# Seven quarter products for eight in the layer-0 gate and up projections of a two-layer diffusion backbone

## The chip, the core and the metric

The kernel runs on one core of one Trainium2 chip. The metric is the time of one execution on the device in microseconds (us). The time before is 2477.42 us, the median of three runs (2466.64 to 2477.6).

The core's engines are called by their short names in the profile: PE is TensorE (matmuls; PEld are its weight loads), DVE is VectorE, ACT is ScalarE, POOL is GpSimd, SP is the engine that issues most transfers here. All of them read and write the on-chip memory SBUF; matmuls write to PSUM.

## The reference, cut to what matters

Two layers work on a residual of 1024 features for 512 main tokens and, in layer 0, 256 context tokens. Each layer norms the residual with a modulation that depends on the conditioning, mixes tokens in three branches, merges them, and ends with a SwiGLU feed-forward network (FFN) of 2816 hidden features:

```python
sh1, sc1, g1, sh2, sc2, g2 = jnp.split(sc @ w_ada[l] + b_ada[l], 6, axis=-1)
h = rmsnorm(x, norm1_g[l]) * (1.0 + sc1) + sh1
y, yc = hybrid_mixer(h, hc, w_in[l], ..., w_branch[l], w_out[l], need_ctx)
x = x + g1 * y
h = rmsnorm(x, norm2_g[l]) * (1.0 + sc2) + sh2
x = x + g2 * ((jax.nn.silu(h @ w_gate) * (h @ w_up)) @ w_down)
```

In layer 0 the same is done for the context tokens, with the same weights; in layer 1 only the main tokens go on. Everything is float32.

## The kernel before

**Matmuls.** Features lie on the 128 partitions and tokens along the columns: 768 columns in layer 0 (512 main, 256 context), 512 in layer 1. To keep float32 accuracy, each operand is split in a high and a low part of a narrower type, and a product is three matmuls: high by high, high by low, low by high. `dense` (L290) makes one output tile of 128 features: it loops over the input tiles `k` (eight for 1024 features) and the three part products, and each of these is one matmul of 512 columns and, in layer 0, a second one of 256 columns, because a PSUM bank holds 512. A gate tile in layer 0 is thus 8 x 3 x 2 = 48 matmuls.

**Weights.** `load_raw` (L275) has SP load a weight tile of up to 128 x 1024 numbers into one of three raw buffers (`wr`, L110). `load_w` (L280) splits it: ScalarE copies the high part (L286, into one of two `wh` buffers), VectorE subtracts (L287, into one of two `wl` buffers). A raw buffer is free again when both have read it, a `wh` or `wl` buffer when the last matmul with it is done. The split of the next tile therefore runs beside the matmuls of this one.

**Order of work.** The order on each engine is made ahead by a scheduler from the program order, with dependences and buffers; it may move an instruction ahead of another on the same engine that is not ready in its estimate. On the chip each engine then works through its list in order. SBUF space for activations comes from 27 pages, each for two row blocks of 768 columns (`Pages`, L61; `pair` takes a whole page, `single` a half), handed out in program order by an estimate of TensorE's clock that `spent` (L316) advances.

**FFN.** `layer` (L1071) runs the FFN in four pieces of 5, 5, 6 and 6 hidden tiles (`FF_PIECES`, L30). For each hidden tile of a piece it makes the gate tile, takes its silu on ScalarE (L1176), makes the up tile, multiplies on VectorE (L1178) and splits the result in high and low parts (`gu`, L576 and L577). The piece ends with eight down products, each over the tiles of the piece, whose result is added to the residual X on VectorE (`add_res`, L624), main and context tokens apart. In the last piece the two token blocks are done one after the other. When the first block is done, `settle` (L500) norms it for what follows while the second block's down products run: squares (ScalarE) and their sums (GpSimd and VectorE, L496), a matmul with ones (L458), a power on GpSimd (L468), spreading over the partitions (L482), and then for each feature tile a scaled copy and its high and low parts (L537 to L547).

**Modulation.** `ada_units` (L371) makes four feature tiles of the modulation vectors in four steps. A step loads 512 KB of `w_ada` through the same three raw buffers and accumulates on VectorE (L368; the first product of a unit on ScalarE, L366); the fourth step folds the result (L343, L344). A double unit serves main and context conditioning, a single one the main one alone. The steps wait in a queue; `fill(n)` (L445) puts n of them at a place in the program, `drain` all that are left. Layer 0's own units 4 to 11 are made during its mixer. At the end of layer 0's merge (L1145) the queue gets layer 1's four double units 0 to 3 (16 steps) and its eight single units 4 to 11 (32 steps). One step follows each hidden tile (L1185) and each down product (L1196) of layer 0's FFN.

**Merge.** Before the FFN, each of 3 x 8 merge steps makes a sigmoid gate tile (`w_in`, 1024 features in) and a branch tile (`w_branch`, 512 features in), and adds their product to `macc` (VectorE for the first branch, then also GpSimd, L1138). `fill(1)` follows each; in layer 1 the queue is empty by then.

## Time and profile before

| what | value |
|---|---|
| median of the runs | 2477.42 us |
| profiled execution, from its first to its last instruction | 2460.2 us |
| PE busy | 2410.8 us (98%) |
| VectorE busy | 1426.7 us (58%) |
| ScalarE busy | 837.1 us (34%) |
| GpSimd busy | 202.6 us (8%) |
| granted TensorE clock, mean | 0.998 |

The profile is of one execution. It has no time of its own beside the span of its instructions; the median of the runs lies 17.2 us above it. Times in the trace are counted from the span's start. A stage row gives a stretch, its length, and then for each engine the busy time with the number of instructions in brackets, followed by the granted clock, the share in which the transfer engines were busy, and GB/s. A group row gives line, engine and operation, output and inputs by the program's names, the shape, the count, busy time and mean duration in ns, and then the engine's idle time before them with what ended it. A row of the order in time gives start, duration, engine and line. Matmul durations overlap their neighbours, so the distance of two starts is what one costs.

### The profile page before, as it was taken

What the parts mean: (1) busy time and instruction counts of PE and PEld (TensorE: products, weight loads), DVE (VectorE), ACT (ScalarE), POOL (GpSimd) and SP (SyncE); (2) the same over time, 40 slices, a digit from 0 to 9 for tenths busy, and PEclk for the clock granted to TensorE, in tenths of its full rate; (3) what the DMA queues carried; (4) which work ended last, traced back from release to release, by engine and by line L of the source; (5) the groups of instructions that cost most, each with busy time, mean ns of one, the idle gap of its engine ahead of it and who ended that gap; (6) DMA issues with size and microseconds to landing.
All of it is one profiled execution on the core that took longest, in us unless ns stands there. A gap on an engine that the chain in (4) does not pass through costs nothing. (4 is left out here: it accounts for less than half of the span.)

```text
span 2460.2 us, 34161 instructions
## 1 busy us (share of the span) xinstructions
PE 2410.8 (98%) x13814; PEld 2074.5 (84%) x13814; DVE 1426.7 (58%) x2452; ACT 837.1 (34%) x1372; POOL 202.6 (8%) x143
## 2 busy tenths in 40 slices
PE   8999999999999999999999999999999999999998
PEld 3888888888888888888888888888888889888888
DVE  4688777875454374745353376668884337434335
ACT  3333344442222342221222253324453335322224
POOL 0000100000111210000000040101000122000001
PEclk9999999999999999999999999999999999999999
DMA  8222111123433243434344351112113335233334
GB/s 293 71 78 78 52 42 37 31 60 108 146 112 90 82 127 97 136 98 144 94 122 118 90 150 58 39 42 60 50 51 107 107 102 160 80 102 101 94 101 131
DMA packets 361869, 236.33 MB, mean 96 GB/s; under 512 B 8112, under 2 KB 333168, under 8 KB 361712
## 3 DMA queue, kind: packets, MB, share of 16 engines
q1 hardware_dynamic: 357776, 221.57, 30.5%
q0 software_dynamic: 2304, 10.49, 1.3%
q8 instruction: 109, 1.79, 0.3%
q10 hardware_dynamic: 1632, 2.10, 0.3%
q14 instruction: 48, 0.39, 0.0%
HBM read 226.78 MB, written 7.34 MB: 95 GB/s over the span
## 5 line engine op out<-in xcount | busy, mean ns | idle before, releaser
L286 ACT ACTIVATE wh<-wr 128x1024 fp32r<-128x1024 f32 (+2 forms) x364 | 344.7, 947 | 1042.7 <-PE pd L304 962.1
L287 DVE TENSOR_TENSOR wl<-wr,wh 128x1024 fp32r<-128x1024 f32 (+2 forms) x364 | 396.3, 1089 | 255.4 <-ACT wh L286 251.8
L304 PE MATMUL pd<-hh,wh 128*128 128x512 f32 (+1 forms) x1504 | 456.6, 359 | 1.0 <-DVE X L624 0.8
L304 PE MATMUL pd<-hh,wl 128*128 128x512 f32 (+1 forms) x1504 | 446.5, 353 | 0.3 <-DVE wl L287 0.3
L304 PE MATMUL pd<-hl,wh 128*128 128x512 f32 (+1 forms) x1504 | 443.9, 351 | 0.0
L304 PE MATMUL pd<-fl,wh 128*128 128x512 f32 (+1 forms) x1072 | 322.3, 352 | 0.0
L304 PE MATMUL pd<-fh,wl 128*128 128x512 f32 (+1 forms) x1072 | 321.8, 351 | 0.3 <-DVE wl L287 0.3
L304 PE MATMUL pd<-fh,wh 128*128 128x512 f32 (+1 forms) x1072 | 321.1, 351 | 0.6 <-ACT silu L1176 0.6
L304 PEld LDWEIGHTS pd<-hh,wl 128*128 128x128 f32 x1504 | 246.7, 188 | 37.6 <-DVE wl L287 0.8
L304 PEld LDWEIGHTS pd<-hl,wh 128*128 128x128 f32 x1504 | 246.5, 189 | 34.0
L304 PEld LDWEIGHTS pd<-hh,wh 128*128 128x128 f32 x1504 | 247.4, 189 | 31.3 <-ACT wh L286 1.2
L368 DVE SCALAR_TENSOR_TENSOR acc<-wra,sc,acc 128x512 f32<-128x512 f32 x224 | 162.1, 755 | 190.5 <-DMA wra<-in_w_ada 140.8
L304 PEld LDWEIGHTS pd<-fh,wl 128*128 128x128 f32 x1072 | 177.6, 188 | 30.0 <-DVE wl L287 1.2
L304 PEld LDWEIGHTS pd<-fh,wh 128*128 128x128 f32 x1072 | 176.9, 188 | 29.3 <-ACT silu L1176 0.8
L304 PEld LDWEIGHTS pd<-fl,wh 128*128 128x128 f32 x1072 | 177.4, 188 | 28.0
L304 PE MATMUL pd<-guh,wl 128*128 128x512 f32 (+1 forms) x576 | 174.8, 340 | 1.1 <-DVE wl L287 1.1
L304 PE MATMUL pd<-guh,wh 128*128 128x512 f32 (+1 forms) x576 | 175.0, 340 | 0.0
L304 PE MATMUL pd<-gul,wh 128*128 128x512 f32 (+1 forms) x576 | 174.5, 339 | 0.0
L1178 DVE TENSOR_TENSOR silu<-pd,silu 128x768 f32<-128x768 f32 (+1 forms) x44 | 36.2, 824 | 164.8 <-PE pd L304 164.8
L624 DVE SCALAR_TENSOR_TENSOR X<-pd,mod,X 128x256 f32<-128x256 f32 (+1 forms) x128 | 65.9, 546 | 94.7 <-PE pd L304 94.6
L304 PEld LDWEIGHTS pd<-guh,wl 128*128 128x128 f32 x576 | 99.5, 189 | 14.2 <-DVE wl L287 1.8
L304 PEld LDWEIGHTS pd<-gul,wh 128*128 128x128 f32 x576 | 99.5, 189 | 12.5
(224 smaller groups left out, 3362.0 us busy)
## 6 DMA issues: line engine op xcount, KB each, us to landing
wr<-in_w_in SPq DMA_DIRECT2D x116, 512.0 KB, 3.8
wra<-in_w_ada SPq DMA_DIRECT2D x80, 512.0 KB, 3.7
wr<-in_w_ffn_gate SPq DMA_DIRECT2D x44, 512.0 KB, 3.8
wr<-in_w_ffn_up SPq DMA_DIRECT2D x44, 512.0 KB, 3.9
wr<-in_w_ffn_down SPq DMA_DIRECT2D x48, 384.0 KB, 3.4
wr<-in_w_out SPq DMA_DIRECT2D x32, 512.0 KB, 4.1
wr<-in_w_branch SPq DMA_DIRECT2D x48, 256.0 KB, 2.8
wr<-in_w_ffn_down SPq DMA_DIRECT2D x32, 320.0 KB, 3.1
```

Source lines behind the costliest of these rows:

```text
L286: nc.scalar.activation(out=h, in_=r, func=AF.Copy)
L287: nc.vector.tensor_tensor(out=o, in0=r, in1=h.bitcast(F32), op=ALU.subtract)
L304: nc.tensor.matmul(ps[:, b0:b1], lhsT=w[:, k, :], rhs=x[:, b0:b1], start=b not in first, stop=(k == kt - 1 and i == 2), skip_group_check=True)
L368: nc.vector.scalar_tensor_tensor(out=acc[:, 0:512], in0=w, scalar=sc, in1=acc[:, 0:512], op0=ALU.mult, op1=ALU.add)
L624: self.nc.vector.scalar_tensor_tensor(out=self.X[m][:, c0:c1], in0=ps[:, c0:c1], scalar=gcol(b, m), in1=self.X[m][:, c0:c1], op0=ALU.mult, ...
L1178: nc.vector.tensor_tensor(out=s[:, 0:tt], in0=pu[:, 0:tt], in1=s[:, 0:tt], op=ALU.mult)
```

## The change

For 20 of the 22 hidden tiles of layer 0's FFN, two neighbouring output tiles are made together, with the input features split in two halves of 512 and the tokens in two halves of 384 (`H`). A 2 x 2 by 2 x 2 block product needs eight quarter products; the change uses the scheme with seven, which needs sums of weight quarters and of activation quarters. A quarter product is 4 x 3 = 12 matmuls of 384 columns.

```diff
-FF_PIECES = (5, 5, 6, 6)
+FF_PIECES = ((4, 4, 4, 4, 4, 2), (5, 5, 6, 6))
+FF_PLAIN = 2
+H = T // 2
...
+    def high_low(self, parts):
+        hi = self.wh.tile([P, KD, P], F32R, tag="wh", name=self.nm("wh"))
+        lo = self.wl.tile([P, KD, P], F32R, tag="wl", name=self.nm("wl"))
...
+            self.nc.scalar.activation(out=h, in_=src, func=AF.Copy)
+            self.nc.vector.tensor_tensor(out=l, in0=src, in1=h.bitcast(F32), op=ALU.subtract)
...
+    def seven_acts(self, act):
...
+        for k in range(KD // 2):
...
+            r1, r2 = self.single("b1"), self.single("b2")
+            for r, h, l in ((r1, h1, l1), (r2, h2, l2)):
+                nc.gpsimd.tensor_tensor(out=r[:, 0:T], in0=h[:, 0:T].bitcast(F32), in1=l[:, 0:T].bitcast(F32),
+                                        op=ALU.add)
...
+            nc.vector.tensor_tensor(out=n1, in0=r1[:, 0:H], in1=r1[:, H:T], op=ALU.subtract)
+            nc.vector.scalar_tensor_tensor(out=n2, in0=r2[:, H:T], scalar=-1.0, in1=n1, op0=ALU.mult,
+                                           op1=ALU.subtract)
+            nc.vector.tensor_tensor(out=t3, in0=r2[:, H:T], in1=r1[:, H:T], op=ALU.subtract)
+            nc.vector.scalar_tensor_tensor(out=t4, in0=n2, scalar=-1.0, in1=r2[:, 0:H], op0=ALU.mult,
+                                           op1=ALU.subtract)
...
+            self.split(n[:, 0:T], nh[:, 0:T], nl[:, 0:T])
+            self.split(t3, t3p[:, 0:H], t3p[:, H:T])
...
+        yield None
+        for k, (t, t4) in enumerate(last):
+            h1, l1 = act[k]
+            self.split(t4, h1[:, H:T], l1[:, H:T])
...
+    def product(self, out, w, k0, xs, start):
...
+        for k in range(KD // 2):
+            xh, xl = xs[k]
+            for i, (a, x) in enumerate(((wh, xh), (wh, xl), (wl, xh))):
+                nc.tensor.matmul(out, lhsT=a[:, k0 + k, :], rhs=x, start=first, stop=(k == KD // 2 - 1 and i == 2),
+                                 skip_group_check=True)
...
+    def seven(self, w1, w2, q, take):
...
+        r1, r2 = (self.load_raw(w, KD).rearrange("p k c -> p (k c)") for w in (w1, w2))
...
+        for o, x, y in ((s1, r2[:, 0:n], r2[:, n:2 * n]), (s2, s1, r1[:, 0:n]), (s3, r1[:, 0:n], r2[:, 0:n]),
+                        (s4, s2, r1[:, n:2 * n])):
+            nc.gpsimd.tensor_tensor(out=o, in0=x, in1=y, op=ALU.add)
...
+        g1 = self.high_low([r1])
+        self.product(al, g1, 0, q["B11"], True)
+        nc.scalar.copy(out=u1, in_=al)
+        self.product(be, g1, KD // 2, q["B21"], True)
+        take(0, 0, be, u1)
+        g2 = self.high_low([s21])
+        self.free(sa)
+        self.product(al, g2, 0, q["N2"], False)
+        nc.scalar.copy(out=u2, in_=al)
+        self.product(ga, g2, KD // 2, q["N1"], True)
+        nc.scalar.copy(out=u5, in_=ga)
+        g3 = self.high_low([s34])
+        self.free(sb)
+        self.product(al, g3, 0, q["T3"], False)
+        take(1, 1, al, u5)
+        self.product(ga, g3, KD // 2, q["B22"], False)
+        take(0, 1, ga, u2)
+        g4 = self.high_low([r2[:, n:2 * n]])
+        self.product(al, g4, 0, q["T4"], False)
+        take(1, 0, al, None)
...
+        if l == 1:
+            self.ada_queue += self.ada_units(1, (4, 5, 6, 7), 1) + self.ada_units(1, (8, 9, 10, 11), 1)
...
-                self.fill(1)
+                self.fill(1 + l)
             self.free(*brheld)
         self.free(*hheld)
+        self.drain()
         if l == 0:
-            self.drain()
-            self.ada_queue += self.ada_units(1, (0, 1, 2, 3), 2) + self.ada_units(1, range(4, 12), 1)
+            self.ada_queue += self.ada_units(1, (0, 1, 2, 3), 2)
...
+                if l == 0 and i == 0:
+                    making = self.seven_acts(act2)
+                    next(making)
+                self.fill(0 if l == 0 else 1)
+            if l == 0:
+                if quarters is None:
+                    quarters, qheld = next(making)
+                self.seven_gate_up(l, range(max(f0, plain), f0 + n, 2), quarters, gu, guheld)
```

In words: the first two hidden tiles are made as before (`FF_PLAIN`). After the first, `seven_acts` forms the activation quarters: for each of four pairs of input tiles two GpSimd sums of 768 columns, four VectorE operations of 384, and splits in high and low parts. The quarter T4 is written over the second token half of the first four input tiles once the plain tiles are done.

`seven` (one call for the gate, one for the up of each pair of tiles) loads both raw weight tiles, has GpSimd make four sums of 512 columns, splits four sets of weights (three of 1024 columns and one of 512) and issues the seven products, sets 1 to 3 for two products each and the fourth for the last. Partial results that are used twice are copied from PSUM by ScalarE (`u1`, `u2`, `u5`). `take` is `gate` or `up` inside the new `seven_gate_up`: for the gate, three VectorE additions of 384 columns and four silus; for the up, three additions and four multiplications on VectorE. The split of the pair's results into `gu` stays as it was.

Layer 0's FFN now has six pieces of 4, 4, 4, 4, 4 and 2 tiles, so 48 down products instead of 32, each over fewer tiles. No modulation step follows a hidden tile there any more; the 16 double steps of layer 1 follow the down products. The 32 single steps of layer 1 move to its own merge, two after each merge step.

More of the change, by code (lines that the diff above doesn't have):

```diff
@@ L336, in finish_chains @@
             self.step_chain()
+    def high_low(self, parts):
+        hi = self.wh.tile([P, KD, P], F32R, tag="wh", name=self.nm("wh"))
+        lo = self.wl.tile([P, KD, P], F32R, tag="wl", name=self.nm("wl"))
+        o = 0
+        for src in parts:
+            n = src.shape[1]
+            h, l = (t.rearrange("p k c -> p (k c)")[:, o:o + n] for t in (hi, lo))
+            self.nc.scalar.activation(out=h, in_=src, func=AF.Copy)
+            self.nc.vector.tensor_tensor(out=l, in0=src, in1=h.bitcast(F32), op=ALU.subtract)
+            o += n
+        return hi, lo
@@ new lines, in product @@
+    def product(self, out, w, k0, xs, start):
+        nc = self.nc
+        wh, wl = w
+        first = start
+        for k in range(KD // 2):
[3 more added lines that the diff above has]
+                                 skip_group_check=True)
+                first = False
+            self.spent(3 * (H / 2400 + 0.0133))
@@ new lines, in seven_gate_up, with combine, gate, up @@
+    def seven_gate_up(self, l, tiles, q, gu, guheld):
+        nc, a = self.nc, self.a
+        col = lambda name, i: a[name][l][:, i * P:(i + 1) * P]
+        for i in tiles:
+            s = self.pair("silu")
+            def combine(out, t, h, x, y):
+                if (t, h) == (1, 1):
+                    nc.vector.scalar_tensor_tensor(out=out, in0=x, scalar=-1.0, in1=y, op0=ALU.mult, op1=ALU.subtract)
+                else:
+                    nc.vector.tensor_tensor(out=out, in0=x, in1=y, op=ALU.add)
+            def gate(t, h, x, y):
+                o = s[:, t, h * H:(h + 1) * H]
+                if y is None:
+                    nc.scalar.activation(out=o, in_=x, func=AF.Silu, scale=-1.0)
+                    return
+                combine(o, t, h, x, y)
+                nc.scalar.activation(out=o, in_=o, func=AF.Silu)
+            def up(t, h, x, y):
+                o = s[:, t, h * H:(h + 1) * H]
+                if y is None:
+                    nc.vector.scalar_tensor_tensor(out=o, in0=x, scalar=-1.0, in1=o, op0=ALU.mult, op1=ALU.mult)
+                    return
+                combine(y, t, h, x, y)
+                nc.vector.tensor_tensor(out=o, in0=y, in1=o, op=ALU.mult)
+            for name, take in (("w_ffn_gate", gate), ("w_ffn_up", up)):
+                self.seven(col(name, i), col(name, i + 1), q, take)
+            hp, lp = self.pair("guh", F32R), self.pair("gul", F32R)
+            guheld.extend([hp, lp])
+            for t in (0, 1):
+                self.split(s[:, t, 0:T], hp[:, t, 0:T], lp[:, t, 0:T])
+                gu.append((hp[:, t, :], lp[:, t, :]))
+            self.free(s)
@@ L1166, in layer @@
         f0 = 0
-        for pi, n in enumerate(FF_PIECES):
-            last = pi == len(FF_PIECES) - 1
+        pieces = FF_PIECES[l]
+        plain = FF_PLAIN if l == 0 else 2 * D_FF
+        quarters = qheld = None
+        for pi, n in enumerate(pieces):
+            last = pi == len(pieces) - 1
             gu, guheld = [], []
-            for i in range(n):
+            for i in range(min(n, max(0, plain - f0))):
                 c0 = (f0 + i) * P
@@ L1184, in layer @@
                 gu.append((hp[:, i % 2, :], lp[:, i % 2, :]))
-                self.fill(1)
+                if l == 0 and i == 0:
[6 more added lines that the diff above has]
+                self.seven_gate_up(l, range(max(f0, plain), f0 + n, 2), quarters, gu, guheld)
             if last:
                 self.free(*hheld)
+                if l == 0:
+                    self.free(*qheld)
             if last and l == 0:
```

31 lines of the change are left out of this document (added).

## The prediction

> **What bounds the kernel now.** I read the page first, then the busy time by stage, the order in time inside a stage, and the groups by shape. The first page lines say who is always busy.
>
> ```profile
> span 2460.2 us, 34161 instructions
> PE 2410.8 (98%) x13814; PEld 2074.5 (84%) x13814; DVE 1426.7 (58%) x2452; ACT 837.1 (34%) x1372; POOL 202.6 (8%) x143
> ```
>
> TensorE (PE) is busy 98% of the span. The stage table shows whether that holds where the change is: the FFN of layer 0 (902.5 to 1462.4) and the branch merge of layer 1 (the last two rows).
>
> ```profile
> core 0: us, PE busy (x) PEld busy (x) DVE busy (x) ACT busy (x) POOL busy (x), PEclk, DMA share, GB/s
> 902.50:988.90 86.40, 85.64 (x487) 73.84 (x486) 48.46 (x71) 23.82 (x34) 1.15 (x1) 1.00 0.36 105
> 989.00:1030.60 41.60, 41.60 (x241) 36.60 (x240) 32.04 (x49) 9.68 (x14) 0.00 (x0) 1.00 0.50 144
> 1156.40:1256.10 99.70, 99.70 (x577) 87.23 (x576) 37.45 (x42) 22.27 (x25) 0.00 (x0) 1.00 0.36 104
> 1439.60:1462.40 22.80, 20.98 (x168) 20.00 (x167) 20.02 (x29) 16.36 (x27) 12.94 (x10) 1.00 0.59 162
> 1827.00:1868.00 41.00, 40.93 (x233) 34.15 (x232) 30.68 (x76) 22.99 (x56) 0.00 (x0) 1.00 0.20 59
> 1887.10:2033.80 146.70, 146.70 (x649) 121.45 (x648) 51.98 (x64) 45.29 (x64) 26.09 (x17) 1.00 0.36 106
> ```
>
> 1156.4 to 1256.1 is the gate and up work of six tiles: PE has no gap, VectorE (DVE) is 38% busy, GpSimd (POOL) idle. So fewer matmuls there shorten the kernel until another engine fills up. Busy time hides what one matmul costs, since neighbours overlap; the start times give it.
>
> ```profile
> 1437.11 0.39 PE L304 MATMUL pd<-gul,wh 128*128 128x512 f32 x1
> ...
> 1439.38 0.39 PE L304 MATMUL pd<-guh,wl 128*128 128x512 f32 x1
> ...
> 1446.05 0.28 PE L304 MATMUL pd<-guh,wh 128*128 128x256 f32 x1
> ...
> 1447.24 0.28 PE L304 MATMUL pd<-gul,wh 128*128 128x256 f32 x1
> ```
>
> Ten starts lie between the first two rows and ten between the last two: 0.227 us per matmul of 512 columns, 0.119 us per one of 256. The mean of the two, 0.173 us, is also 99.7 / 576 in the stage table. A matmul of 384 columns lies midway, so I take 0.173 us for it.
>
> **Term A, matmuls removed.** A pair of gate (or up) tiles takes 96 matmuls now, 96 x 0.173 = 16.6 us. Seven products of 12 matmuls with 384 columns take 84 x 0.173 = 14.5 us, 2.08 us less. Twenty tiles make ten pairs, gate and up, so 20 calls: -41.6 us. By the Trainium skill (TensorE: Matmul & The Clock Gate, "Back-to-back issue gap"), a warm matmul costs its columns over 2.4 GHz plus 2.5 ns; that gives 0.216 and 0.109 us where the trace has 0.227 and 0.119, and the saving, an estimate from that page, would be 39 us.
>
> Everything else is cost. Its prices come from the groups by shape.
>
> ```profile
> L287 DVE TENSOR_TENSOR wl<-wr,wh 128x1024 fp32r<-128x1024 f32 x236 | 289.2, 1225 | 239.4 <-ACT wh L286 235.9 <-PE pT L949 0.5
> L286 ACT ACTIVATE wh<-wr 128x1024 fp32r<-128x1024 f32 x236 | 250.1, 1060 | 733.7 <-PE pd L304 659.1 <-issue 69.9 <-ACT sq L494 2.6
> L287 DVE TENSOR_TENSOR wl<-wr,wh 128x512 fp32r<-128x512 f32 x48 | 34.4, 716 | 0.0
> L1138 POOL TENSOR_TENSOR macc<-macc,gt 128x512 f32<-128x512 f32 x16 | 26.3, 1641 | 106.0 <-DVE gt L1135 106.0
> L662 POOL TENSOR_TENSOR Y<-K 128x768 f32<-128x768 f32 x4 | 8.1, 2018 | 0.0
> L577 DVE TENSOR_TENSOR gul<-silu,guh 128x768 fp32r<-128x768 f32 x22 | 21.0, 953 | 0.5 <-ACT guh L576 0.4
> L368 DVE SCALAR_TENSOR_TENSOR acc<-wra,sc,acc 128x512 f32<-128x512 f32 x224 | 162.1, 755 | 190.5 <-DMA wra<-in_w_ada 140.8 <-ACT acc L366 48.8
> L344 DVE TENSOR_REDUCE parts<-tr 128x16 f32<-128x512 f32 x32 | 20.9, 670 | 0.3
> L343 DVE STREAM_TRANSPOSE tr<-acc 128x512 f32<-128x512 f32 x32 | 21.4, 693 | 0.3
> L624 DVE SCALAR_TENSOR_TENSOR X<-pd,mod,X 128x512 f32<-128x512 f32 x32 | 24.0, 749 | 42.2 <-PE pd L304 42.2
> L624 DVE SCALAR_TENSOR_TENSOR X<-pd,mod,X 128x256 f32<-128x256 f32 x96 | 44.0, 479 | 52.5 <-PE pd L304 52.3
> ```
>
> **Term B, inside a call.** Per pair of tiles (29.1 us of PE) VectorE has six weight subtractions of 1024 and two of 512 (8.8 us), two of 768 for the split of the result (1.9), and ten operations of 384 columns on the products' results, 0.48 each by half of 953 ns (4.8): 15.5 us. GpSimd has eight sums of 512, 13.1 us; its queue holds nothing else here (0.00 in the rows of this FFN until the last norm). ScalarE has eight weight copies of at most 1.06 us and twelve smaller operations of at most 0.8 us (the silu row in term C): below 20 us. All fit in time; the order decides. With two buffers each for high and low weights, the first weights of the next call reuse those of products 5 and 6, so they can be made only during product 7, 2.08 us. They take 1.06 + 1.225 = 2.29 us, and the low part is first read by the third matmul, 0.35 us later: 2.43 us are available. 0.14 us is spare, and nothing may stand in front. Every other pair of weights has two products, 4.2 us. What can stand in front is a GpSimd sum:
>
> ```profile
> 1450.25 1.30 POOL L543 TENSOR_TENSOR hl<-nt,hh 128x512 fp32r<-128x512 f32 x1 [1.04 <-ACT hh L542]
> ...
> 1450.74 1.62 DVE L287 TENSOR_TENSOR wl<-wr,wh 128x768 fp32r<-128x768 f32 x1
> ...
> 1454.47 0.95 DVE L287 TENSOR_TENSOR wl<-wr,wh 128x768 fp32r<-128x768 f32 x1
> ```
>
> The same subtraction takes 0.95 us alone and 1.62 us beside a GpSimd addition: it starts late by the rest of it. GpSimd is busy 6.6 of 14.5 us per call; met at random, a sum is running 45% of the time with half its 1.64 us left, 0.37 us per call. But the sums for the next call can start when its second raw tile has landed (its buffer is freed about 0.5 us into this call, plus 3.8 us of landing) and so lie mostly ahead of product 7. I take 0.2 x 20 = +4 us, with bounds 0 and a whole sum each time, 33 us. Here and below nothing lies under 0: none of the added work replaces PE work, and PE has no gap there to win back.
>
> **Term C, making the activation quarters.** Eight GpSimd sums of 768 (16.1 us), and on VectorE two differences and one low part for each of four pairs before product 3 can start (4 x 1.9 = 7.6), beside six weight subtractions (7.4) and four operations of the two plain tiles (3.8): 35 us, one after another if they exclude each other. They need all columns of h:
>
> ```profile
> L1176 ACT ACTIVATE silu<-pd x44: 576/686/797, 917.8 to 2408.9; 128x768 f32<-128x768 f32 x22, 128x512 f32<-128x512 f32 x22
> ```
>
> The first silu, hence a first gate tile complete with its context columns, comes at 917.8. Product 3 is due at 902.5 + 33.2 (four plain products) + 4.2 + about 3 (the loss in that row) = 943, 25 us later. Short by 10 us at most; some weight work is ahead of it. I take +5 us, bounds 0 and 10.
>
> **Term D, down products.** Six pieces instead of four need as many matmuls, 22 x 8 x 6. The 16 double modulation steps, earlier spread over tiles and down products, now all fall into the first two pieces. One costs 14/16 of four accumulations (2.64) and a quarter of two folds (0.68): 3.3 us, beside a low part of 512 (0.72) and two residual additions (1.23): 5.25 us of VectorE per 4.16 us of PE, 17 us over 16 products. The row at 989.0 had the same steps beside 5.2 us products and PE lost nothing, so some backlog is absorbed ahead. I take +2, bounds 0 and 17. The other 32 steps leave this FFN; VectorE was not its limit, so that brings nothing.
>
> **Term E, the last piece and layer 1's norm.** The second block of the last piece covers the norm of the first:
>
> ```profile
> 1442.12 1.05 PE L458 MATMUL st<-ones,sqa 128*128 128x1 f32 x8
> ...
> 1465.19 2.39 POOL L543 TENSOR_TENSOR hl<-nt,hh 128x512 fp32r<-128x512 f32 x1 [2.87 <-ACT hh L542]
> ```
>
> From the sums to the last low part the norm takes 25.5 us. The cover was 144 matmuls of 0.119 = 17.1 us; with two tiles it is 48, 5.7 us. Cover lost: 11.4 us. VectorE has eight smaller weight splits meanwhile (768 to 256 columns, about 0.5 us each, 4 us), which shortens the norm: 7.4 us, and 0.6 for the two result tiles that the first product waits for: +8 us, bounds 4 and 13.
>
> **Term F, modulation in layer 1.** Two single steps follow each of 16 merge steps of 146.7 / 18 = 8.15 us. Loads share three raw buffers:
>
> ```profile
> wr<-in_w_in SPq DMA_DIRECT2D x116, 512.0 KB, 3.8
> wra<-in_w_ada SPq DMA_DIRECT2D x80, 512.0 KB, 3.7
> wr<-in_w_branch SPq DMA_DIRECT2D x48, 256.0 KB, 2.8
> ```
>
> A buffer is held 3.8 + 1.06 + 1.225 = 6.1 us by a gate weight, about 4.2 by a branch weight, 3.7 + 1.5 = 5.2 by each step: 20.7 us through three buffers is 6.9 of 8.15 us. It fits while landing stays so short at twice the traffic. In the first four merge steps VectorE is already busy 30.7 of 41 us, and eight steps at 1.66 (two accumulations, an eighth of them on ScalarE, and a quarter fold) add 13.3: 3 us over. I take +5, bounds 0 and 14.
>
> **Sum.** -41.6 + 4 + 5 + 2 + 8 + 5 = -17.6 us: the span goes from 2460.2 to 2442.6 us. The median, 2477.4, stands 17.2 us above that span; unchanged, that gives 2459.8, say 2460 us, 0.7% faster. A measurement here can tell about 0.5%, 12.4 us.
>
> **Rivals.** *Everything is hidden*: terms B to F stay near their lower bounds, 4 to 8 us in all; about 2441 us. For it: PE lost nothing at 75% VectorE load. Against: the norm's cover is shorter in any case.
>
> *The gain is eaten*: terms B to F at half of their upper bounds, 33 + 10 + 17 + 13 + 14 = 87 us, so 43 us against 41.6: about 2479 us. For it: each added piece lands on VectorE, GpSimd or the three raw buffers in a place with little slack. Against: the terms would all have to go badly, each for its own reason. It would end in the same place if 384-column matmuls went slower than midway between the two measured sizes; nothing between 256 and 512 columns is in this trace, but a straight line through both leaves little room.
>
> *Slower, by the port at the end of each call*: a GpSimd sum stands before the low part of the next call's first weights in every call, and a 384-column operation queued before it waits too: 1.64 + 0.48 = 2.1 us per call, 42 in place of 4: +20 us, about 2498 us. It decides from 1.7 us per call on, (41.6 - 20 + 12.4) / 20. For it: 0.14 us of slack, and VectorE operations with two inputs in SBUF (8.8 + 1.9 + three of 0.48) plus GpSimd fill 12.1 + 13.1 of 29.1 us. Against: GpSimd's work can lie early in the call. This is what the Trainium skill says (SBUF — State Buffer, "Who interferes with whom"): a VectorE operation with two SBUF inputs and a GpSimd operation exclude each other for a whole instruction. By that rule the delay is a whole remainder, as in the rows at 1450; the trace agrees.
>
> **How the numbers follow.** Forecast 0.42, all hidden 0.20, gain eaten 0.22, slower 0.16. Faster by over 0.5%: the first two, less a little of the forecast's slow edge, 0.60; within 0.5%: 0.24; slower: 0.16. The range starts at the whole of term A, 2436, and reaches past the eaten gain to 2487; only most of the slower rival lies beyond.
>
> **What would show it.** Right: 384-column matmuls starting every 0.173 us; calls of 14.6 to 15 us; a gap of some 5 us before the first third product; PE idle about 8 us more around layer 1's first norm; merge steps of layer 1 near 8.4 us. Wrong: calls beyond 16 us with weight subtractions stretched beside GpSimd sums (the slower rival), 384-column starts well above 0.173 us, or PE waits on modulation loads in layer 1 above 14 us.

## The result

The change made the kernel slower: 2582.74 us (median of 4 runs, 2580.78 to 2584.96) against 2472.03 us for the kernel before on the same chip (2465.76 to 2477.6, 4 runs). The ratio is 1.0456, with a 95% interval of 1.0428 to 1.0484. Forecast were 2460 us and a range up to 2487 us, so the result lies far outside, on the other side. One run of an experiment below (8502 us, of the kernel with its sums on VectorE) stands apart from the three others of its kernel and is left out.

The profiled execution of the changed kernel spans 2583.0 us, 122.8 more than the one of before. The medians are 110.7 us apart; the profiled execution of before, 2460.2 us, was shorter than every run of that kernel on record (from 2463.33 us on). The first page lines of the changed kernel:

```profile
span 2583.0 us, 34315 instructions
PE 2428.9 (94%) x13582; PEld 2088.2 (81%) x13582; DVE 1549.7 (60%) x2648; ACT 904.4 (35%) x1520; POOL 325.6 (13%) x231
```

TensorE has 232 matmuls fewer in the profile, but is busy 94% of a longer span instead of 98%: it waits now. The stage table of the changed kernel says where. The columns are those of the table in the prediction; the first five rows are from layer 0's FFN (the plain tiles; two calls and their down products; four calls; the down products of a piece; the last down products), then come layer 1's mixer and its merge, and at the end four calls of a later piece.

```profile
core 0: us, PE busy (x) PEld busy (x) DVE busy (x) ACT busy (x) POOL busy (x), PEclk, DMA share, GB/s
908.90:963.20 54.30, 40.10 (x200) 32.56 (x199) 40.88 (x55) 17.52 (x30) 21.83 (x13) 0.87 0.17 50
963.20:1035.80 72.60, 65.34 (x362) 58.01 (x360) 50.75 (x77) 22.10 (x33) 5.72 (x4) 1.00 0.34 102
1156.90:1237.90 81.00, 66.13 (x348) 60.34 (x347) 35.76 (x64) 25.87 (x39) 22.63 (x16) 0.98 0.18 52
1346.30:1379.40 33.10, 33.10 (x193) 28.97 (x193) 15.32 (x25) 6.48 (x10) 4.47 (x4) 1.00 0.29 84
1525.00:1555.60 30.60, 25.19 (x121) 18.66 (x119) 24.63 (x41) 17.76 (x37) 16.03 (x16) 0.94 0.49 157
1555.60:1927.70 372.10, 358.57 (x2136) 307.65 (x2135) 275.75 (x532) 155.73 (x293) 36.14 (x22) 0.99 0.18 53
1927.70:2156.80 229.10, 217.74 (x975) 174.42 (x974) 144.87 (x236) 78.33 (x136) 26.29 (x19) 0.98 0.55 162
...
1270.90:1346.30 75.40, 63.14 (x339) 57.99 (x338) 31.68 (x40) 25.81 (x39) 18.47 (x14) 1.00 0.17 48
```

In the last row four calls take 75.4 us, 18.85 each, although VectorE and ScalarE are each busy less than half of the time and GpSimd a quarter; before, a pair of tiles took 16.6 us. Stage by stage, before and after (starts of the first matmul of each stage):

| stage | before | after | difference |
|---|---|---|---|
| up to the FFN of layer 0 | 902.5 | 908.9 | +6.4 |
| FFN of layer 0 | 560.1 | 646.7 | +86.6 |
| mixer of layer 1 | 365.4 | 372.1 | +6.7 |
| merge of layer 1 | 206.1 | 229.1 | +23.0 |
| the rest | 426.2 | 426.2 | 0.0 |

The first difference lies ahead of everything that the change touches. It follows none of the edits below: in the traces of the experiments the same stretch takes between 902 and 910 us. Its cause is open.

What holds a call up stands in the order in time of the changed kernel, one call of a gate, its TensorE rows at each wait with the rows of what they wait for (in brackets the idle time before the instruction and what ended it):

```profile
1295.46 0.33 PE L405 MATMUL pa<-nl,wh 128*128 128x384 f32 x1
1295.63 0.34 PE L405 MATMUL pa<-nh,wl 128*128 128x384 f32 x1
1296.01 0.48 ACT L440 COPY ptmp<-pa 128x384 f32<-128x384 f32 x1 [1.15 <-PE pa L405]
1296.54 0.45 PE L405 MATMUL pa<-nh,wh 128*128 128x384 f32 x1 [0.57 <-ACT ptmp L440]
...
1299.81 0.61 PE L405 MATMUL pa<-t3p,wh 128*128 128x384 f32 x2 [0.91 <-ACT ptmp L442]
...
1302.30 0.56 DVE L463 SCALAR_TENSOR_TENSOR ptmp<-pa,ptmp 128x384 f32<-128x384 f32 x1 [2.19 <-PE pa L405]
1302.91 0.44 PE L405 MATMUL pa<-fh,wh 128*128 128x384 f32 x1 [0.73 <-DVE ptmp L463]
...
1305.33 0.56 DVE L465 TENSOR_TENSOR ptmp<-pa,ptmp 128x384 f32<-128x384 f32 x1 [1.88 <-PE pa L405]
1305.94 0.44 PE L405 MATMUL pa<-fh,wh 128*128 128x384 f32 x1 [0.65 <-DVE ptmp L465]
```

The first two rows start 0.17 us apart, as was predicted for 384 columns. Then the first matmul of product 4 comes 0.91 us after the last one of product 3 instead of 0.17. Product 4 writes `ga`, and the copy of `al` (L440), which it doesn't touch, is what it waits for. The same happens ahead of products 5, 6 and 7: each waits for the reader of the product before it. `al` and `ga` are the two halves of one PSUM tile, `pa`. No engine is slow here: ScalarE and VectorE read as soon as the product is done, and their 0.5 us, which nothing covers, are the larger part of each wait.

### The profile page after: what moved, and what is told of

The parts are those of the page before. It is cut to its first block, busy times and chain, and to the rows that moved or that the text cites. A ratio compares the mean times of both kernels' runs of the same rounds, so it can differ in the third digit from the quotient of the medians.

```text
span 2583.0 us, 34315 instructions
## 1 busy us (share of the span) xinstructions
PE 2428.9 (94%) x13582; PEld 2088.2 (81%) x13582; DVE 1549.7 (60%) x2648; ACT 904.4 (35%) x1520; POOL 325.6 (13%) x231
## 5 line engine op out<-in xcount | busy, mean ns | idle before, releaser
L288 ACT ACTIVATE wh<-wr 128x1024 fp32r<-128x1024 f32 (+4 forms) x340 | 301.7, 888 | 850.3 <-PE pd L306 604.1
L289 DVE TENSOR_TENSOR wl<-wr,wh 128x1024 fp32r<-128x1024 f32 (+4 forms) x340 | 350.7, 1033 | 209.0 <-ACT wh L288 205.7
L306 PE MATMUL pd<-fl,wh 128*128 128x512 f32 (+1 forms) x432 | 160.7, 379 | 5.7 <-DVE fl L701 5.7
L306 PE MATMUL pd<-fh,wl 128*128 128x512 f32 (+1 forms) x432 | 160.2, 378 | 5.9 <-DVE wl L289 5.8
L306 PE MATMUL pd<-fh,wh 128*128 128x512 f32 (+1 forms) x432 | 159.3, 377 | 2.8 <-DVE silu L1337 2.2
L778 DVE SCALAR_TENSOR_TENSOR X<-pd,mod,X 128x256 f32<-128x256 f32 (+1 forms) x160 | 84.0, 559 | 111.5 <-PE pd L306 111.3
L306 PEld LDWEIGHTS pd<-guh,wh 128*128 128x128 f32 x576 | 98.1, 190 | 23.9 <-ACT wh L288 10.3
L405 PE MATMUL pa<-fh,wh 128*128 128x384 f32 x240 | 85.5, 356 | 24.9 <-DVE ptmp L463 7.3
L1294 POOL TENSOR_TENSOR macc<-macc,gt 128x768 f32<-128x768 f32 (+1 forms) x32 | 60.3, 1884 | 337.7 <-DVE gt L1291 331.1
L650 POOL TENSOR_TENSOR sqa<-sqa,sq 128x256 f32<-128x256 f32 (+1 forms) x40 | 50.8, 1269 | 412.5 <-ACT sq L648 412.4
```

Source lines behind the costliest of these rows:

```text
L288: nc.scalar.activation(out=h, in_=r, func=AF.Copy)
L289: nc.vector.tensor_tensor(out=o, in0=r, in1=h.bitcast(F32), op=ALU.subtract)
L306: nc.tensor.matmul(ps[:, b0:b1], lhsT=w[:, k, :], rhs=x[:, b0:b1], start=b not in first, stop=(k == kt - 1 and i == 2), skip_group_check=True)
L405: nc.tensor.matmul(out, lhsT=a[:, k0 + k, :], rhs=x, start=first, stop=(k == KD // 2 - 1 and i == 2), skip_group_check=True)
L650: eng.tensor_tensor(out=acc[:, c0:c1], in0=acc[:, c0:c1], in1=sq[:, c0:c1], op=ALU.add)
L778: self.nc.vector.scalar_tensor_tensor(out=self.X[m][:, c0:c1], in0=ps[:, c0:c1], scalar=gcol(b, m), in1=self.X[m][:, c0:c1], op0=ALU.mult, ...
```

## The experiments

The first theory: the program's waits go by the tile and not by the half of it that is read, so every product from the fourth on waits for a reader of the other half. The first rival: the port shared by VectorE and GpSimd delays the weights (the prediction's slower case). Four edits of the changed kernel came first. Each run is compared with the kernel before on the same chip, as a ratio; a difference "by the ratios" is that of two ratios, times 2472 us.

**A tile of its own for `ga`.**

```diff
-        al, ga = ps[:, 0:H], ps[:, 512:512 + H]
+        al = ps[:, 0:H]
+        ga = self.bank("pg")[:, 0:H]
```

> One edit to the changed kernel: the third accumulator of a call (ga) gets a PSUM tile of its own instead of the second bank of the tile that holds the first one (al). Theory 1: in the changed kernel a call takes 18.8 us instead of 14.6 because product 4 waits for the copy of al, product 5 for the copy of ga, product 6 for the reader of al and product 7 for the reader of ga: the program's waits go by the PSUM tile, not by the bank, so each reader of one accumulator holds the next product on the other. With tiles apart, no product has to wait for the reader of the product just before it: calls of 14.6 to 15.5 us, 20 x 3.5 to 4.2 = 70 to 84 us less, about 2500 to 2513 us, still slower than before. Rival: the copies and subtractions themselves come too late (one product is too short a cover, or GpSimd's sums hold VectorE); then the waits stay, on other readers, and the time stays within 20 us of 2583.

2507.92 us, ratio to before 1.0136 (1.0115 to 1.0157). The stretch of four calls, and the place in time that answers to the one above:

```profile
1230.40:1289.40 59.00, 58.90 (x338) 58.09 (x337) 32.61 (x39) 25.11 (x39) 18.94 (x14) 1.00 0.20 58
```

```profile
1250.82 0.33 PE L405 MATMUL pa<-nh,wh 128*128 128x384 f32 x1
1251.00 0.33 PE L405 MATMUL pa<-nl,wh 128*128 128x384 f32 x1
1251.17 0.33 PE L405 MATMUL pa<-nh,wl 128*128 128x384 f32 x1
1251.34 0.33 PE L405 MATMUL pg<-nh,wh 128*128 128x384 f32 x1
```

TensorE goes from product 3 to product 4 in 0.17 us, and four calls take 59.0 us instead of 75.4: 14.75 each, of which 14.53 are matmuls. The twenty calls of the FFN take 308.0 us instead of 388.4. That settles the theory. The GpSimd sums are all still there, so the rival is out; a weight subtraction of 1024 columns beside them takes some 1.4 us instead of 1.225, and all that is left in a steady call beside its matmuls is 0.22 us:

```profile
L350 DVE TENSOR_TENSOR wl<-s,wh 128x1024 fp32r<-128x1024 f32 x8 | 11.2, 1398 | 4.3 <-ACT wh L349 4.3
L426 POOL TENSOR_TENSOR s<-s,wr 128x512 f32<-128x512 f32 x7 | 10.2, 1462 | 0.2
```

`al` and `ga` lie in different PSUM banks in both kernels. The Trainium skill (PSUM — Partial Sum Buffer, "PSUM bank collisions raise a hardware error") asks for a guard by bank and quadrant, and not by address. This run agrees as far as banks go: the first product into `pg` starts 0.17 us after the last matmul into `pa`, with the copy of `pa` still to come. A guard by a tile of two banks is coarser than that. The wait was one that the program made, not one that the memory needed.

The kernel is still 1.4% slower than before, so the other terms were wrong too.

**No seven products at all**, all 22 tiles plain, with the six pieces and the new places of the modulation kept (`FF_PLAIN = 22`, and no `seven_acts` nor `seven_gate_up`).

> The changed kernel without the seven products: all 22 hidden tiles of layer 0 are made as before, in the six pieces of 4, 4, 4, 4, 4 and 2, with the modulation steps as in the change. It gives the price of the pieces and of the moved modulation by themselves. Expected against the kernel before: last piece and norm +7, first two down phases +8, layer 1's merge +23, its mixer 0 to +7: 38 to 45 us slower, 2510 to 2520 us. If instead most of the change's 110 us were due to the pieces and the modulation and not to the calls, it would lie near 2560 or above.

2520.42 us, 1.0188 (1.0162 to 1.0214), just above the expected 2510 to 2520. So the pieces and the moved steps alone cost 1.9%; the seven products of the changed kernel, which should have saved 1.7%, cost another 2.6%. The merge took 229.1 us, as in the changed kernel.

**The single modulation steps back in layer 0's FFN**, two after each down product from the third piece on.

> One part of the changed kernel undone: the 32 single modulation steps of layer 1 go back into layer 0's FFN (two after each down product of pieces 3 and on, behind the 16 double ones), none in layer 1's merge. Theory: the merge of layer 1 took 229.1 us instead of 206.1 because four loads per merge step go through three raw buffers; without the steps it returns to 206 to 208, 21 to 23 us less, and the FFN of layer 0 gains 0 to 12 us of waits in its down products: net 10 to 23 us faster than the changed kernel, 2560 to 2573. Rival: the merge is slower for another reason (half the TensorE clock after gaps, another order); then it stays above 220 us.

2599.32 us, 1.0505 (1.0482 to 1.0528): slower, a miss. Two rows of down products with the steps, and the last one layer 1's merge:

```profile
1234.30:1283.40 49.10, 38.23 (x192) 31.25 (x191) 39.37 (x61) 8.54 (x13) 0.00 (x0) 0.93 0.68 206
1362.10:1409.90 47.80, 37.74 (x193) 30.16 (x191) 39.10 (x61) 8.53 (x13) 0.00 (x0) 0.96 0.73 212
...
1965.20:2171.40 206.20, 206.00 (x959) 170.87 (x958) 90.14 (x147) 73.97 (x128) 27.62 (x19) 1.00 0.34 100
```

The merge has its old time and TensorE is busy all through it, so the steps were all of its 23 us. But 33.1 us of down products became 48 to 49, with VectorE busy 39 of them. In the first of these rows ScalarE's copies of weights waited 14.8 us in all for accumulations and 11.7 us for loads of down weights, so VectorE's work and the loads through the raw buffers both hold the products up; which of the two is the limit isn't shown. The place that the change had cleared was no free place any more, because the down products of a piece of four are short.

**The sums of 768 columns on VectorE instead of GpSimd** (L370), against the rival that the port makes the loss in the plain tiles.

> One edit to the changed kernel: the eight sums of 768 columns that make the activation quarters run on VectorE instead of GpSimd. In the changed kernel the four plain products took 54 us instead of 36: three low parts of the context columns of h, 0.48 us each alone, took 2 us each beside the GpSimd sums, TensorE had gaps of 1.2 to 5.9 us and then half its clock. Theory: with GpSimd's sums gone the low parts are short again; VectorE has 8 x 0.95 = 7.6 us more of its own, so the stretch falls to 40 to 46 us: 8 to 14 us faster than the changed kernel, 2569 to 2575. Rival: the stretch is long because VectorE has too much to do there in any case; then it stays at 52 us or more.

2576.85 us (median of three), 1.0432 (1.0403 to 1.046): 6 us better than the changed kernel by the medians and by the ratios, where 8 to 14 were expected. The plain tiles still take 51.1 us, close to the rival's 52 and far from the theory's 40 to 46. In the changed kernel GpSimd did hold VectorE up; in its order in time on VectorE, the low parts of 256 columns (L701), two in the row at 925, take 2 us each while sums run:

```profile
925.09 3.98 DVE L701 SCALAR_TENSOR_TENSOR fl<-nt,mod,fh 128x256 fp32r<-128x256 f32 x2
...
944.58 1.21 DVE L289 TENSOR_TENSOR wl<-wr,wh 128x1024 fp32r<-128x1024 f32 x1
```

With the sums on VectorE two of them take 0.88 us, yet TensorE's longest wait grew, from 5.5 to 12.3 us, as these rows of that experiment show, VectorE's and then TensorE's:

```profile
916.29 0.88 DVE L701 SCALAR_TENSOR_TENSOR fl<-nt,mod,fh 128x256 fp32r<-128x256 f32 x2
917.08 0.95 DVE L370 TENSOR_TENSOR b<-fh,fl 128x768 f32<-128x768 f32 x1
917.95 0.56 DVE L374 TENSOR_TENSOR n<-b 128x384 f32<-128x384 f32 x1
...
936.19 1.22 DVE L289 TENSOR_TENSOR wl<-wr,wh 128x1024 fp32r<-128x1024 f32 x1
```

```profile
937.46 1.01 PE L306 MATMUL pd<-fh,wl 128*128 128x512 f32 x2 [12.29 <-DVE wl L289]
```

From 917 to 936 VectorE's list holds the making of the quarters, nearly without a break, and only then the low part of the weights of a plain tile (L289). In the changed kernel the same weights (the row at 944.58) stand behind the same work: a weight that TensorE needs now is queued behind work that it needs later. The run with the sums on VectorE also gave it 7.6 us more to do, so it doesn't say what the shared port alone costs. The theory for the second half of the loss is the order on VectorE, in all the places where the change puts work on it. The next runs all start from the kernel with `ga` in its own tile (1.0136). The intervals of the single edits overlap with its interval, so each gain is read from the stages too.

**The quarters made after the second plain tile** (`if l == 0 and i == 1`), not the first.

> On the kernel with ga in its own PSUM tile: the making of the activation quarters stands after the second plain tile in the program instead of after the first. Theory: TensorE waited 5.9 us for low weights and 4.1 us for an up product's reader because the making's operations stood before them on VectorE, and 4 us for the low parts of h that GpSimd's sums held; standing later in the program they yield to the plain tiles, and the loss moves to the third product of the first call, which then waits 5 to 12 us. In all 3 to 10 us faster than 2507.9. Rival: the same loss or a larger one at the first call, no change or slower.

2494.94 us, 1.0098 (1.0072 to 1.0124): 13 us faster by the medians, 9 by the ratios. The plain tiles fall from 54.7 to 44.3 us, of which 33.2 are matmuls, and the first two calls rise from 29.3 to 31.2, by less than the 5 to 12 us expected there.

**A double modulation step after every second down product** of pieces 1 to 4 (`fill(m % 2)`), not after every one of pieces 1 and 2.

> On the kernel with ga in its own PSUM tile: the 16 double modulation steps of layer 0's FFN follow every second down product of pieces 1 to 4 instead of each one of pieces 1 and 2. Theory: in pieces 1 and 2 VectorE has 5.25 us of work per 4.16 us product, the down phases take 39 us instead of 33.3 and the calls behind them start 5 to 8 us late (64 and 67 us instead of 59); with half the rate it has 3.6 us per product, and all down phases take 33.3 to 35 us and the calls 59 to 61: 18 to 24 us faster than 2507.9. Rival: the raw buffers, not VectorE's total, hold the products; then each step still costs about 1 us and the gain is under 10 us.

2490.97 us, 1.0086 (1.0057 to 1.0116): 17 us faster by the medians, 12 by the ratios, 10.5 in this FFN; 18 to 24 were expected. In its first piece with steps and the calls behind it:

```profile
987.10:1021.00 33.90, 33.90 (x195) 29.39 (x194) 26.40 (x43) 7.23 (x11) 0.33 (x1) 1.00 0.48 139
1021.00:1083.80 62.80, 59.70 (x338) 57.98 (x337) 34.00 (x40) 25.17 (x39) 23.88 (x16) 1.00 0.20 60
```

The down products lose nothing (39.0 and 38.5 us with a step after each). The calls behind them take 61 to 63 us in all four pieces, against 64.0 and 67.1 in two and 59 in the others: what a piece's down products cannot absorb is still paid in the next calls, but it is less. This run halves the loads as well as VectorE's work per product, so it doesn't separate the two.

**The short piece first, not last**, with no step in it (pieces of 2, 4, 4, 4, 4, 4).

> On the kernel with ga in its own PSUM tile: pieces of 2, 4, 4, 4, 4 and 4 tiles, the piece of two plain tiles first, no modulation step in it. Theory: (a) the norm before layer 1 gets 48 more matmuls of cover: last piece plus layer 1's mixer 14 us nearer to the kernel before; (b) making the activation quarters has the first down products as cover, but VectorE's list is as it was, so of the 18 us lost in the plain tiles 5 to 10 come back. In all 14 to 22 us faster than 2507.9: 2486 to 2494. Rival: the order that the scheduler makes, not the cover, holds TensorE; then (b) gives nothing and the time is near 2494 to 2500.

2499.52 us, 1.0109 (1.0083 to 1.0135), 8 us faster by the medians, 7 by the ratios. The last down products lose 5 us (38.4 where 33.3 are matmuls) instead of 14, and the mixer of layer 1 takes 370.1 us. The plain tiles did not gain (53.9 us), so that part of the expectation failed, and the time is the rival's (2494 to 2500).

**The single steps of the merge in pages, not in the raw buffers**, and, as its control, both only from the second branch on.

> On the kernel with ga in its own PSUM tile (2507.9 us): in layer 1's merge the modulation steps start with the second branch, and their loads go to pages of the activation space instead of the three raw weight buffers. Theory: there the merge was 21 us longer because a gate weight's load can start only when an accumulation has freed a raw buffer (it landed 7 us after ScalarE began to wait for it); with buffers of its own the modulation costs nothing there: merge of layer 1 206 to 210 us instead of 226.9. Rival: VectorE's accumulations or the doubled traffic itself make it longer; then it stays above 218 us.

> Control of the run with modulation loads in pages: the same start of the modulation steps with the second branch, but loads through the three raw buffers. Both theories: a merge of 220 to 232 us, since only the place of the steps differs from the kernel with ga in its own tile.

The merge took 220.1 us with pages and 227.3 in the control, so the raw buffers were about 7 of the 21 us, not all of them; the expected 206 to 210 missed. (In one run each, the times were 2501.94 and 2503.3 us. In the traces with all 32 steps in the merge and the loads through the raw buffers, the merge takes 226.9 to 231.7 us, so a difference of a few us is not resolved.) What the other 14 are was open. Two runs that leave work out, each run once, took the steps apart. (A first form of the second, with one load kept in a page of its own, had no page left for it and gave no time.)

**The loads without the accumulations** (8 of 512 columns left), and **the accumulations without the loads**:

```diff
-                self.ada_accum(state["accs"], raw[:, k, :], 2 * q + k)
+                c = state["accs"][0][:, 0:8]
+                nc.vector.scalar_tensor_tensor(out=c, in0=raw[:, k, 0:8], ...)
...
+                self.ada_accum(state["accs"], self.src[k][0][:, 0:512].bitcast(F32), 2 * q + k)
```

> On top of the gate sums' own tile, whose merge of layer 1 took 226.9 us against 206.1 before the change. The 32 single steps keep their loads through the three raw buffers, but of VectorE's accumulations only 8 of 512 columns are left (the rest of the sums is left out, and the first product on ScalarE stays). If most of the 21 us are the accumulations on VectorE's list, with the gate and branch weights queued behind them, the merge falls to 207 to 214 us. If the raw buffers and the doubled traffic make most of it, it stays at 216 to 225 us.

> The other half of the run that kept the loads: the single steps keep all their arithmetic but read activations that lie in SBUF anyway, so all 32 of their loads are left out and no raw buffer is held for them (the modulation's values are not the right ones). With the loads alone the merge took 218.4 us, 12 over the 206.1 of before and 8 under the whole. If the two halves add, the accumulations alone give 206 + 8 to 9 = 214 to 216 us. If they only cost together (a step late by its load pushes the weights behind it), it falls to 206 to 210 us. If the accumulations alone suffice, it stays above 220 us.

Their merge rows, of the one and then of the other:

```profile
1853.80:2072.10 218.30, 212.24 (x975) 171.36 (x974) 114.68 (x236) 78.41 (x136) 27.43 (x19) 1.00 0.57 170
```

```profile
1852.70:2064.80 212.10, 209.85 (x975) 173.70 (x975) 137.44 (x236) 79.16 (x136) 27.46 (x19) 0.99 0.33 97
```

218.3 and 212.1 us, 12.2 and 6.0 over the 206.1 of before; together 18.2 of 20.8. The two halves add, within 3 us, and the loads are the larger one: neither of the two theories had it all. The split isn't quite clean, since the short accumulations that are left in the first run still make VectorE wait for their loads, 19.5 us in all. How the loads cost that is seen in the changed kernel, in the waits of ScalarE and the medians from issue to landing in its merge:

```profile
ACT wh L288 <- DMA wr<-in_w_in: 56.1, 10, 7.6
```

```profile
wra<-in_w_ada SPq DMA_DIRECT2D x30, 512.0 KB, 3.8
wr<-in_w_in SPq DMA_DIRECT2D x22, 512.0 KB, 4.8
wr<-in_w_branch SPq DMA_DIRECT2D x23, 256.0 KB, 3.9
```

ScalarE waited ten times for a gate weight, up to 7.6 us; in the merge of before it waited for none. A gate weight lands 1.1 us later after its issue than there (3.7). Its issue waits for a raw buffer as it did before, and now stands among the steps' loads in SP's list, which waited 29 times for an accumulation, 37.9 us in all. How this reaches TensorE is seen in the order in time, ScalarE's rows and then TensorE's:

```profile
2039.36 1.06 ACT L288 ACTIVATE wh<-wr 128x1024 fp32r<-128x1024 f32 x1 [6.81 <-DMA wr<-in_w_in]
2040.32 0.58 ACT L1282 ACTIVATE gt<-pd 128x512 f32<-128x512 f32 x1
```

```profile
2040.95 0.50 PE L306 MATMUL pd<-hh,wh 128*128 128x512 f32 x1 [2.09 <-ACT gt L1282]
```

ScalarE stands 6.8 us at the copy of a late gate weight. Behind it in its list is the read of a finished gate tile (L1282), and TensorE waits for that read before it writes `pd` again. Six of TensorE's waits in this merge end so, 7.2 us of 11.

**A middle way**: 24 single steps after the down products of pieces 3 to 5, 8 in the merge.

> On the kernel with ga in its own PSUM tile: of the 32 single modulation steps, 24 follow the down products of pieces 3 to 5 of layer 0's FFN, one each, and 8 stay in layer 1's merge, one after each step of the second branch. Theory: one single step (512 KB, 1.66 us of VectorE) beside a down product of 4.16 us costs under 0.5 us, where two cost 2 us in the run with all steps back in layer 0; merge 206 to 211 us instead of 226.9, the three down phases 33.3 to 37 us each: 6 to 20 us faster than 2507.9. Rival: any load that shares the three raw buffers with products of 4.16 us delays them; then the three down phases take 40 us or more each and nothing is won.

2500.55 us, 1.0119 (1.0093 to 1.0146), 7 us faster by the medians and 4 by the ratios, which is not clear of the noise: the merge fell to 213.4 us, but the calls behind the steps rose by 2.3 to 3.3 us per piece. Even one step per down product isn't free there.

**The three edits together**: quarters later, short piece first, double steps after every second down product.

> The three edits that each gained alone on top of the gate sums' own tile, together: the quarters made after the second plain tile (13 us faster alone), double modulation steps after every second down product (17 us alone), the short piece first instead of last (8 us alone, 3 of it lost again in the last piece). If the places are independent, 2508 - 13 - 17 - 8 = 2470 us (2464 to 2478), about the time of the kernel before: layer 0's FFN about 535 us, the last piece below 36 us. If they share VectorE's slack, so that the steps that leave the down products queue up behind the later making of the quarters, the sum fails and it stays at 2480 to 2490. The merge of layer 1 stays at 226 to 229 us under both.

2471.15 us, 1.0001 (0.9988 to 1.0014). The gains add up as expected; the time is that of the kernel before. Layer 0's FFN takes 536.8 us, 23 less than before, and the merge, at 228.8, gives all of it back. The mixer takes 373.4 us, 8 more than before.

**With the single steps in layer 1's mixer**, eight after each HGRN head.

> As the run before it, with the 32 single modulation steps taken out of layer 1's merge and put into layer 1's mixer, eight after each HGRN head. The merge then has the steps of the kernel before and takes 206 us (204 to 208) under every theory. If the mixer has room on the engines that a step uses (its loads, the split on ScalarE and VectorE, three narrow products of some 0.2 us each on TensorE), it grows by no more than 5 us and the sum is 2450 to 2460 us, faster than before. If each step costs there what it cost in the merge (about 0.7 us a step), the mixer grows by 15 to 25 us and the time stays within 5 us of the run before it.

2457.65 us, 0.9948 (0.9932 to 0.9964): 0.5% faster than the kernel before, 13 us under it. Its stages (plain tiles, four calls, down products with steps, last down products, mixer, merge):

```profile
902.10:946.30 44.20, 37.75 (x200) 31.04 (x200) 39.78 (x55) 16.79 (x30) 16.66 (x9) 0.96 0.09 27
...
1154.20:1213.50 59.30, 58.95 (x339) 58.05 (x338) 32.49 (x41) 26.31 (x40) 21.51 (x15) 1.00 0.22 63
1213.50:1247.40 33.90, 33.90 (x193) 29.37 (x193) 26.83 (x43) 7.03 (x11) 1.89 (x2) 1.00 0.48 140
1400.80:1438.70 37.90, 36.87 (x218) 32.21 (x217) 27.37 (x44) 22.59 (x40) 15.91 (x16) 1.00 0.63 188
1438.70:1820.10 381.40, 363.29 (x2152) 312.24 (x2151) 323.73 (x618) 159.32 (x300) 29.96 (x23) 0.98 0.32 94
1820.10:2026.30 206.20, 205.99 (x959) 170.76 (x958) 90.02 (x147) 73.73 (x128) 27.63 (x19) 1.00 0.34 100
```

The mixer grew by 8 us for 32 steps, 0.25 us a step where the merge paid 0.7. The mixer's growth lies between the two cases that had been put down; the time is that of the first.

## Why the prediction was wrong, term by term

The table goes by the profiles of the two kernels; what the calls lose is split by the kernel with `ga` in its own tile. It uses 0.173 us for every 384-column matmul. A call is its 84 matmuls, 14.53 us.

| term | predicted | measured | what it was |
|---|---|---|---|
| A, matmuls removed | -41.6 | -41.6 | starts are 0.173 us apart |
| B, inside a call | +4 (0 to 33) | +80 and +4 | waits by tile: 388.4 - 308.0 us; the rest, 0.22 us in a steady call |
| C, quarters | +5 (0 to 10) | +18 | plain tiles 54.3 us, against 33.2 + 3 before |
| D, double steps | +2 (0 to 17) | +21 | 8 in the down products of pieces 1 and 2, 13 in the calls behind them (with `ga` in its own tile) |
| E, last piece and norm | +8 (4 to 13) | +14 | 7 in the last down products, 7 at the start of the mixer |
| F, single steps in the merge | +5 (0 to 14) | +23 | loads 12, accumulations 6 of 21, by the two halves |

With the 6.4 us ahead of the FFN these give 125, and 122.8 were measured; the FFN of before had some 2 us of small losses in other places that the table doesn't take off.

**The step that failed is in term B.** The prediction wrote "All fit in time; the order decides", and then looked only at the weights of the next call. It never asked, for each product, what must have read its output tile before it may be written, so these waits stood at nothing in the sum; they measured 80 us. The kernel's text held the answer: `al` and `ga` are cut from one tile `ps`, and each is read right after the product that ends it, first by ScalarE and then by VectorE. Four waits of 0.57 to 0.91 us, in the rows above, go with calls 4.1 us longer (18.85 against 14.75). The slower rival had the right sign for the wrong reason: subtractions did stretch beside the sums (1.4 us for 1.225), but with the sums in place all that a steady call lost was 0.22 us, 4 us in twenty. That this equals the 4 us that term B gave to the port is luck as far as the runs show: none of them says what the 0.22 us are.

**Terms C, D and F were priced in one way**, by adding up busy time and comparing it with TensorE's: 35 us of work for the 25 until product 3 in C, 5.25 of 4.16 with an absorbed backlog in D, 30.7 of 41 in F. But what TensorE waits for is one weight or one tile, and what delays it is what stands ahead in another engine's list, or a load that comes late. In C the loss lay in the plain tiles and not ahead of product 3. C had also left out half of the making: VectorE's list holds all four differences of a pair and two low parts (in the changed kernel 0.54 to 0.94 us each, some 3.6 us a pair) where C counted 1.9, and nearly all of it stood ahead of a plain tile's weights. D shows both: in the first piece with steps ScalarE waited 14.8 us for loads of down weights and 6.4 us for an accumulation, in the kernel with `ga` in its own tile. Against the rival "The gain is eaten" the prediction said that the terms would all have to go badly, each for its own reason. In the kernel with `ga` in its own tile they did go badly together, and the time went past even that rival's 2479 us. C, D and F load the same engines and, D and F, the same three buffers, at places with little slack; their risks were not separate ones.

F named its own condition, that landing stays as short at twice the traffic: it went from 3.7 to 4.8 us, and ten gate weights came late.

**E** had the right mechanism and was short by half. The lost cover showed in the down products (30.6 us for 16.6 of matmuls; the kernel before lost 6.6 there), but the norm's tail reached into the mixer as well (one of its first matmuls waited 1.9 us for the norm), and there TensorE was at half clock (below). With four tiles in the last piece the down products lost 5 us, yet the mixer still took 370.1 us: its share doesn't go with the cover alone, and what else it needs is open.

The median was taken as the sum plus 17.2 us. Most of that offset was spread between executions: for the runs whose span is on record the time is some 2 us above the span (2584.96 and 2583.0 for the changed kernel), so the profiled execution of before was a short one.

## What to carry over

Before a saving in matmuls is counted, go through the output tiles and ask what the writer of each must wait for: in this kernel two independent halves of one tile were one thing to the program's waits. A reader that nothing covers cost TensorE at least its whole length, each time. And slack on an engine at 40% load isn't room for more work: what counts is what will stand ahead of the next weight in its list, and extra terms on the same lists and buffers can go wrong together.

## What the hardware showed

The granted clock fell behind long waits of TensorE, and what followed took nearly twice as long. In the changed kernel it was at half in these three windows, among others; in the first, TensorE works without a break:

```profile
929.80:933.20 3.40, 3.40 (x10) 2.62 (x9) 3.40 (x2) 2.28 (x3) 3.07 (x2) 0.50 0.00 0
940.00:950.20 10.20, 4.69 (x15) 3.76 (x14) 8.73 (x14) 2.74 (x5) 0.28 (x1) 0.50 0.25 72
1557.80:1568.00 10.20, 7.41 (x18) 5.56 (x19) 7.17 (x14) 4.04 (x7) 7.07 (x4) 0.50 0.40 112
```

The prediction had no price for that; by an estimate from these rows, half of TensorE's busy time in the first two, some 4 us, is part of term C's 18. Matmuls of 512 columns start 0.43 us apart in the first window instead of 0.227:

```profile
931.32 0.63 PE L306 MATMUL pd<-fl,wh 128*128 128x512 f32 x1
931.75 0.63 PE L306 MATMUL pd<-fh,wl 128*128 128x512 f32 x1
932.17 0.63 PE L306 MATMUL pd<-fh,wh 128*128 128x512 f32 x1
```

TensorE was busy 1.31 us of the 3.4 us ahead of the first and of the third window, and 1.17 ahead of the second. The windows are 3.4 us or a multiple of it, and their starts lie on one grid: 929.8, 940.0 and 1557.8 are 3 and 181 times 3.413 us apart. By the Trainium skill (TensorE: Matmul & The Clock Gate, "Part 1: The HAM clock gate (the "warmup" mystery)") the activity window is 3413 ns and runs freely; the records here agree in both. The waits of 0.6 to 0.9 us in the calls, four in each 18.9 us, did not lower the clock in the row of four calls at 1270.9: it stands at 1.00, with TensorE busy 63.14 of 75.4 us. So the clock had no part in the 4 us per call.

A VectorE operation with two inputs in SBUF stretches beside GpSimd: 256 columns took 2 us instead of 0.44 while sums of 768 ran, five of which took 10.14 us, 2.03 each. By the Trainium skill (SBUF — State Buffer, "Who interferes with whom") the two exclude each other, and this agrees. TensorE's four waits for these low parts, 1.2 to 1.84 us each, are part of what the plain tiles lost; with the sums on VectorE, and so with more work there, the stretch was 3 us shorter.
